# Seven products of block sums in place of eight, in the first product of a feed-forward layer

## The chip, the core and the metric

The kernel runs on one core of a Trainium2 chip. The core has a matrix engine (TensorE; PE in the profile, and PEld for its weight loads), a vector engine (VectorE, DVE), a scalar engine (ScalarE, ACT), a general engine (GpSimd, POOL) and a sync engine (SyncE, SP), which here issues the large transfers. Each engine works through its own queue in order; they wait for each other by semaphores. The metric is the device time of one execution in microseconds (us), as the median of several runs.

## The reference

A trunk of two pre-norm residual layers works on 256 tokens of 2048 dimensions, in float32. Layer 0 mixes tokens by retention and neighbourhood attention, layer 1 by differential attention. Each layer then has cross-attention into 256 memory tokens and a gated feed-forward block (FFN). Only the FFN bears on the change:

```python
D_MODEL = 2048
SEQ = 256
FFN_HIDDEN = -((-8 * D_MODEL) // (3 * 256)) * 256   # 5632

def swiglu_ffn(h, w_in, w_out):
    g, u = jnp.split(h @ w_in, 2, axis=-1)
    return (jax.nn.silu(g) * u) @ w_out
...
x = x + swiglu_ffn(rms_norm(x, norm_ffn_g[i]), w_ffn_in[i], w_ffn_out[i])
```

So per layer the first product is 256 x 2048 times 2048 x 11264 (gate and up, 5632 columns each), and the second 256 x 5632 times 5632 x 2048.

## The kernel before, in words

**Units.** All large products are cut in the same way. The columns of a weight matrix are taken in blocks of 512 (`NB`), its rows in quarters of 512. One block of one quarter, 128 partitions x 4 x 512 float32 or 1 MB, is loaded into a tile `raw` (three buffers) by one transfer on SP's queue (line 282). A unit is one half of such a tile, two row tiles of 128. `prepare` (line 269) makes each unit's two operands: ScalarE writes the rounded high part `wh` (line 292), VectorE the remainder `wl` (line 293), each 128 x 1024. `wh` and `wl` have three buffers each, and `LOOK = 2` lets `prepare` run two units ahead of the matmuls.

**Matmuls.** `gemm` (line 297) runs the units in the order that `plan` holds. For one unit it does 12 matmuls of 128 x 128 by 128 x 512: for two halves of the tokens (`t`), two row tiles (`j`), and three terms, high x high, high x low and low x high (lines 321 to 323). A block of the first FFN product takes 8 units (the 16 row tiles of 2048 dimensions) and accumulates into two PSUM banks, one for each half of the tokens; then `epi` is called. PSUM has eight banks: pools `ps_acc` (four, tags `acc0` and `acc1`), `ps_t` (two, tag `pt`) and `ps_a` (two, tag `pa`).

**FFN.** The 11 hidden blocks go in three groups of 4, 4 and 3 (`FFN_GROUPS`). In each group the first product alternates a gate block and an up block; `epi_in` (line 841) applies SiLU to the gate block on ScalarE (line 847) and multiplies the up block into it on VectorE (line 850). The result is turned by `act_T` (line 830): VectorE transposes 32 x 32 squares (line 389), SP writes it to a DRAM scratch (`zd`, line 391), POOL reads it back regrouped (line 394), and ScalarE and VectorE split it into high and low parts `aT` (lines 429 and 430). Then comes the group's second product. In the first group of a layer the first four blocks run together (`by_rows`, line 229; `wide`), quarter by quarter, since the normalized input `hTf` is itself still being turned: block 0 of it by matmul transposes (`feed_turns`, line 399), blocks 1 to 3 by the same path through DRAM (`feed`, line 409; blocks 2 and 3 use the tiles `qT` and `kT` of the attention stage, which are free in the FFN).

**Order.** Work beside the units is written as small generators that `Side` steps through after each unit (`pump`), or at once when a unit needs them (`drain`, through `gate`). That is the order in which the program writes instructions. A scheduler then lays out each engine's queue, SP's transfers among them.

Of the kernel before, what the change touches and what calls it, by code (L numbers as in the profile page):

```python
# [16 lines left out]
P = 128  # L17
# [64 lines left out]
def trunk_kernel(  # L82
# [181 lines left out]
    units = [(i, b, u) for i, ph in enumerate(plan) for b, u in ph[3]]  # L264
    ahead = deque()
    raws = {}
    at = {"unit": 0, "phase": 0}

    def prepare():

        i, b, u = units[at["unit"]]
        w2, rows, cols, _ = plan[i]
        c, h = u // 2, u % 2
# [22 lines left out]

    def gemm(kts, src, epi, gate=None, steps=1, wide=False):
        hi, lo = src
# [4 lines left out]
        for b, u in order:  # L303
            side.drain((gate or {}).get(u, ()))
            if b not in accs:
                pools = ((ps_acc, f"acc{t}") for t in range(2))
# [4 lines left out]
            while len(ahead) <= LOOK and at["unit"] < len(units):  # L311
                prepare()
            wh, wl = ahead.popleft()
            acc = accs[b]
            first, left[b] = left[b] == nu, left[b] - 1
            last = left[b] == 0
            for t in range(2):
                ts = slice(t * P, (t + 1) * P)
                for j in range(2):
                    kt = kts[u // 2] + 2 * (u % 2) + j  # L320
                    nc.tensor.matmul(acc[t], lhsT=hi[:, kt, ts], rhs=wh[:, j], start=first and j == 0, stop=False)  # L321
                    nc.tensor.matmul(acc[t], lhsT=hi[:, kt, ts], rhs=wl[:, j], start=False, stop=False)  # L322
                    nc.tensor.matmul(acc[t], lhsT=lo[:, kt, ts], rhs=wh[:, j], start=False, stop=last and j == 1)  # L323
            if last:
                epi(b, acc)
            side.pump(steps)

    def rsqrt_mean(dst, ss, n):
# [48 lines left out]
    def regroup(srcs, room=""):  # L377
# [5 lines left out]
        elif room:  # L383
            zt, zT = (qk.tile([P, 4 * T], F32, tag=room + x, name="zz") for x in "hl")
        else:
# [12 lines left out]

    def feed_turns(dst, b, u, srcs, gi, layer, ssr):

# [4 lines left out]
        square_sum(ssr[0][:, u, b:b + 1], srcs[u])  # L405
        return
        yield

# [69 lines left out]
    def turned(name):  # L478
        return tuple(qk.tile([P, 4, T], F32R, name=name + x) for x in "hl")

# [278 lines left out]
    for layer in range(2):  # L759
# [57 lines left out]
        ssr = new_ss("ssx")  # L817
        tasks = []

        def epi_xo(b, acc):  # L820
            add_x(acc, b)
            if b == 0:
                tasks.extend(side.add(feed_turns(hT, b, u, x_block(b), 3, layer, ssr), u) for u in range(2))
            else:
# [11 lines left out]
        for g0, g1 in FFN_GROUPS:  # L836
# [3 lines left out]

            def epi_in(i, acc):
# [11 lines left out]

            gemm(KT4, hT, epi_in, gate=gate, wide=g0 == 0)
            gate = None
# [55 lines left out]
```

## Time and profile before

| | before |
|---|---|
| median of 3 runs (range) | 2474.95 us (2474.5 to 2476.11) |
| profiled execution: time / span of its instructions | 2475.84 us / 2474.1 us |
| PE busy, matmuls | 2456.3 us, 11184 |
| PEld busy | 2037.1 us |
| DVE busy | 1475.7 us |
| ACT busy | 1187.0 us |
| mean granted TensorE clock | 1.000 |
| read from HBM | 486.88 MB, 206 GB/s over the span |

The span runs from the first to the last instruction of the profiled execution; 1.7 us of that execution's time lie around it. Busy time of an engine is the time in which at least one of its instructions runs. A matmul's shown duration is longer than the distance to the next one, since matmuls overlap; the distance of their starts is the rate. The same holds, to a smaller degree, for VectorE and ScalarE: instructions with no wait between them start a little before the one ahead of them has ended.

### The profile page before, as it was taken

The numbers are of one execution on the slowest core, as the hardware profiler recorded it, in microseconds if no ns is written. First come the engines' busy times: TensorE is split into PE (matmuls) and PEld (weight loads), VectorE is DVE, ScalarE is ACT, GpSimd is POOL, SyncE is SP. The second block draws the span as 40 slices with busy tenths as digits, with TensorE's granted clock in tenths as the row PEclk, the third lists the DMA queues.
The fourth block names the chain that finished last, engine by engine and source line by source line (L and its number), as shares of the span: only waits on it lengthen the run. The fifth ranks groups of instructions, "written<-read, shape, count | busy, mean of one in ns | idle before, by whom it ended". The sixth has DMA issues, their size and how long they took to land.

```text
span 2474.1 us, 28641 instructions
## 1 busy us (share of the span) xinstructions
PE 2456.3 (99%) x11184; PEld 2037.1 (82%) x11184; DVE 1475.7 (60%) x1833; ACT 1187.0 (48%) x1538; POOL 138.2 (6%) x215
## 2 busy tenths in 40 slices
PE   8999999999999999999999999999999999999999
PEld 6888888888888888888888888888888888888887
DVE  6775565675655555555567766767655545555554
ACT  6554464564443444444455555655544444443443
POOL 1000001010000000000010000010100000000000
PEclk9999999999999999999999999999999999999999
DMA  8555567656765666566674555675766656665665
GB/s 288 177 169 179 175 226 245 214 192 213 233 216 200 205 212 225 194 198 226 225 241 164 170 170 168 212 249 171 237 222 210 215 188 214 228 206 200 207 217 175
DMA packets 250184, 511.82 MB, mean 207 GB/s; under 512 B 11328, under 2 KB 11968, under 8 KB 250048
## 3 DMA queue, kind: packets, MB, share of 16 engines
q1 hardware_dynamic: 239568, 484.47, 58.5%
q0 software_dynamic: 8320, 23.08, 4.1%
q10 hardware_dynamic: 2160, 2.44, 0.3%
q8 instruction: 87, 1.43, 0.2%
q14 instruction: 49, 0.40, 0.0%
HBM read 486.88 MB, written 23.07 MB: 206 GB/s over the span
## 4 chain that ended last, share of the span: by engine, by line
PE 92%; DMA 3%; DVE 3%; ACT 1%; POOL 1%; issue 0%; ACTq 0%; SPq 0%; POOLq 0%; DVEq 0%
PE acc L322 30%; PE acc L321 30%; PE acc L323 30%; DMA zz<-zd 2%; DVE wl L293 1%; DMA zd<-zz 1%; PE pt L345 1%; ACT wh L292 0%; PE pt L545 0%; PE pa_s L437 0%; PE pa_s L436 0%; DVE x_sb L741 0%; PE pa_s L435 0%; POOL zz L394 0%; PE pa_r L595 0%
## 5 line engine op out<-in xcount | busy, mean ns | idle before, releaser
L293 DVE TENSOR_TENSOR wl<-raw,wh 128x1024 fp32r<-128x1024 f32 (+1 forms) x865 | 1053.7, 1221 | 870.8 <-ACT wh L292 870.4
L292 ACT CAST wh<-raw 128x1024 fp32r<-128x1024 f32 (+1 forms) x865 | 909.1, 1051 | 1158.2 <-PE acc L323 1132.8
L322 PE MATMUL acc<-wl,hTfh 128*128 128x512 f32 x1408 | 547.9, 389 | 0.6 <-DVE wl L293 0.6
L323 PE MATMUL acc<-wh,hTfl 128*128 128x512 f32 x1408 | 547.7, 389 | 0.0
L321 PE MATMUL acc<-wh,hTfh 128*128 128x512 f32 x1408 | 547.7, 389 | 0.0
L321 PE MATMUL acc<-wh,hTh 128*128 128x512 f32 x832 | 332.0, 399 | 9.8 <-ACT wh L292 8.3
L322 PE MATMUL acc<-wl,hTh 128*128 128x512 f32 x832 | 325.7, 391 | 0.9 <-DVE wl L293 0.9
L323 PE MATMUL acc<-wh,hTl 128*128 128x512 f32 x832 | 325.8, 392 | 0.0
L322 PEld LDWEIGHTS acc<-wl,hTfh 128*128 128x128 f32 x1408 | 264.3, 188 | 56.2 <-DVE wl L293 1.4
L323 PEld LDWEIGHTS acc<-wh,hTfl 128*128 128x128 f32 x1408 | 264.3, 188 | 54.9
L321 PEld LDWEIGHTS acc<-wh,hTfh 128*128 128x128 f32 x1408 | 264.3, 188 | 54.9
L322 PE MATMUL acc<-wl,aTh 128*128 128x512 f32 x704 | 274.0, 389 | 0.2 <-DVE wl L293 0.2
L323 PE MATMUL acc<-wh,aTl 128*128 128x512 f32 x704 | 273.9, 389 | 0.0
L321 PE MATMUL acc<-wh,aTh 128*128 128x512 f32 x704 | 273.9, 389 | 0.0
L321 PEld LDWEIGHTS acc<-wh,hTh 128*128 128x128 f32 x832 | 157.2, 189 | 40.0 <-ACT wh L292 8.3
L323 PEld LDWEIGHTS acc<-wh,hTl 128*128 128x128 f32 x832 | 156.7, 188 | 34.0
L322 PEld LDWEIGHTS acc<-wl,hTh 128*128 128x128 f32 x832 | 157.2, 189 | 31.2 <-DVE wl L293 1.8
L394 POOL DMA_DIRECT2D zz<-zd x160 | 87.3, 552 | 1589.9 <-DMA zd<-zz 1410.9
L322 PEld LDWEIGHTS acc<-wl,aTh 128*128 128x128 f32 x704 | 132.1, 188 | 28.2 <-DVE wl L293 0.8
L321 PEld LDWEIGHTS acc<-wh,aTh 128*128 128x128 f32 x704 | 132.1, 188 | 27.5
L323 PEld LDWEIGHTS acc<-wh,aTl 128*128 128x128 f32 x704 | 132.1, 188 | 27.3
L321 PE MATMUL acc<-wh,oTh 128*128 128x512 f32 x256 | 100.2, 392 | 0.0
(189 smaller groups left out, 1940.3 us busy)
## 6 DMA issues: line engine op xcount, KB each, us to landing
raw<-in_w_ffn_in SPq DMA_DIRECT2D x176, 1024.0 KB, 5.1
raw<-in_w_ffn_out SPq DMA_DIRECT2D x88, 1024.0 KB, 5.1
raw<-in_w_in_ab SPq DMA_DIRECT2D x55, 1024.0 KB, 5.2
raw<-in_w_in_c SPq DMA_DIRECT2D x48, 1024.0 KB, 5.2
zd<-zz SPq DMA_DIRECT2D x40, 512.0 KB, 3.8
zz<-zd POOLq DMA_DIRECT2D x160, 128.0 KB, 5.4
raw<-in_w_out_ab SPq DMA_DIRECT2D x16, 1024.0 KB, 5.1
raw<-in_w_xkv SPq DMA_DIRECT2D x16, 1024.0 KB, 5.0
```

Of the source, the lines that this page charges most:

```text
L292: nc.scalar.copy(wh[:, js], raw[:, rs])
L293: nc.vector.tensor_sub(wl[:, js], raw[:, rs], wh[:, js])
L321: nc.tensor.matmul(acc[t], lhsT=hi[:, kt, ts], rhs=wh[:, j], start=first and j == 0, stop=False)
L322: nc.tensor.matmul(acc[t], lhsT=hi[:, kt, ts], rhs=wl[:, j], start=False, stop=False)
L323: nc.tensor.matmul(acc[t], lhsT=lo[:, kt, ts], rhs=wh[:, j], start=False, stop=last and j == 1)
L345: nc.tensor.transpose(pt[:, j, t * P:(t + 1) * P], srcs[t][:, c:c + P], ident)
L394: nc.gpsimd.dma_start(zT[32 * j:32 * j + 32].rearrange("a (i n) -> a i n", i=4), zd[:, :, j].rearrange("i a n -> a i n"))
```

## The change

In a gate block and its up block, one quarter of the 2048 dimensions (the first 512 rows of the weights) is no longer multiplied as eight products of half of the tokens x 256 dimensions x 512 columns, but as seven. The 2 x 2 blocks are: rows of A, the two halves of the tokens; columns of A and rows of B, the even and the odd row tiles of the quarter; columns of B, the gate block and the up block. The form is Strassen's in Winograd's order: four sums of blocks of A (`s1` to `s4`), four of B (`t1` to `t4`), seven products, and sums of the products. It is used for all pairs except the four blocks that run together at the start of a layer: two, four and three pairs in the groups of a layer, 18 in all.

- `by_pairs` gives the order: of the twelve usual units that a pair keeps, two come first, then seven products alternate with seven units, then the last three units.
- `load_seven` loads the quarter of gate and of up, 1 MB each, into the tiles `qT` and `kT` in place of `raw`; these tiles, two of 4 KB per partition each before, become one of 8 KB. The two loads are written six and four units ahead of the pair's first product, counted in units of `prepare`.
- `prepare_seven` makes `wh` and `wl` for each of the seven products, and, after four of them, one block difference in place in the loaded tile, on VectorE.
- `seven` does six matmuls for a product. Three products add into the pair's own accumulators, four have a bank each. Pairs change sides: one has its accumulators in the four banks of `ps_acc` and the single products in `ps_t` and `ps_a`, the next the other way round.
- `combine` takes the single products out of PSUM at three points: one ScalarE copy and four VectorE additions for a pair. `epi_in` then adds them to the two accumulators of each block, four more VectorE additions, before SiLU and the product.
- `feed_turns` has a second step: for block 0 of the normalized input it makes the sums `s1` to `s4` and splits them into high and low parts, once a layer, which all pairs of the layer use.

```diff
+    def by_pairs(nblocks, lead):
+        seq = by_rows(lead, lead) if lead else []
+        for b in range(lead, nblocks, 2):
+            std = [(b + x, 2 * c + h) for c in (1, 2, 3) for x in range(2) for h in range(2)]
+            seq += std[:2]
+            for p in range(7):
+                seq += [(b, ("seven", p)), std[2 + p]]
+            seq += std[9:]
+        return seq
...
-            phase(w_ffn_in[layer], K4, cols, by_rows(n, 4) if g0 == 0 else None)
+            phase(w_ffn_in[layer], K4, cols, by_pairs(n, 4 if g0 == 0 else 0))
...
+    for n, (i, b, u) in enumerate(units):
+        if u == ("seven", 0):
+            sevens[n - 6], sevens[n - 4] = (i, b, 0), (i, b, 1)
...
+    def load_seven(i, b, x):
+        w2, rows, cols, _ = plan[i]
+        raw = seven_raw[x] = qk.tile([P, 4, NB], F32, tag=("qT", "kT")[x], name="raw7")
+        nc.sync.dma_start(raw, w2[rows[0]:rows[0] + 512, cols[b + x]:cols[b + x] + NB].rearrange(
+            "(k p) n -> p k n", p=P))
+    def prepare_seven(p):
+        (b11, b21), (b12, b22) = ([r[:, :, j] for j in range(2)] for r in (
+            seven_raw[x].rearrange("p (h j) n -> p h j n", j=2) for x in range(2)))
+        t1, t3, t2, t4 = b11, b12, b22, b21
+        src = (b11, b22, b21, t1, t3, t2, t4)[p]
+        wh = hip.tile([P, 2, NB], F32R, name="wh")
+        wl = lop.tile([P, 2, NB], F32R, name="wl")
+        nc.scalar.copy(wh, src)
+        nc.vector.tensor_sub(wl, src, wh)
+        if p == 0:
+            nc.vector.tensor_sub(t1, b12, b11)
+        elif p == 1:
+            nc.vector.tensor_sub(t3, b22, b12)
+        elif p == 3:
+            nc.vector.tensor_sub(t2, b22, t1)
+        elif p == 4:
+            nc.vector.tensor_sub(t4, b21, t2)
...
+    def seven(p, b, accs, weights, src, sums, places):
+        wh, wl = weights
+        name = ("p1", "p3", "p2", "p5", "p7", "p6", "p4")[p]
...
+        for h in range(2):
...
+            nc.tensor.matmul(acc, lhsT=lh, rhs=wh[:, h], start=own and h == 0, stop=False)
+            nc.tensor.matmul(acc, lhsT=lh, rhs=wl[:, h], start=False, stop=False)
+            nc.tensor.matmul(acc, lhsT=ll, rhs=wh[:, h], start=False, stop=own and h == 1)
+    def combine(b, u):
...
+        if (b % 2, u) == (1, 2):
+            first = new()
+            nc.scalar.copy(first, pure["p1"])
...
+        elif (b % 2, u) == (1, 5):
+            u2, v = new(), new()
+            add(u2, pure["p6"], combined[0][0])
+            add(v, pure["p5"], u2)
...
+        elif (b % 2, u) == (0, 6):
+            u3 = combined[0][1]
+            add(u3, pure["p7"], u3)
+            w = new()
+            add(w, pure["p5"], u3)
...
-    def feed_turns(dst, b, u, srcs, gi, layer, ssr):
+    def feed_turns(dst, b, u, srcs, gi, layer, ssr, sums):
...
+        a = att.tile([P, 2, T], F32, tag="att", name="parts")
+        for j in range(2):
+            nc.scalar.activation(a[:, j], pt[:, j], AF.Copy, scale=gain(gi, layer, 4 * b + 2 * u + j))
+        (a11, a21), (a12, a22) = ([a[:, j, t * P:(t + 1) * P] for t in range(2)] for j in range(2))
...
+        nc.vector.tensor_tensor(s1, a21, a22, op=ALU.add)
+        nc.vector.tensor_tensor(s2, s1, a11, op=ALU.subtract)
+        nc.vector.tensor_tensor(s3, a11, a21, op=ALU.subtract)
+        nc.vector.tensor_tensor(s4, a12, s2, op=ALU.subtract)
+        sums[u] = tuple(pp.tile([P, 4, P], F32R, tag="p" + x, name="s" + x) for x in "hl")
+        split(*sums[u], s)
...
-        return tuple(qk.tile([P, 4, T], F32R, name=name + x) for x in "hl")
+        both = qk.tile([P, 2, 4, T], F32R, tag=name, name=name)
+        return both[:, 0], both[:, 1]
...
+                if more:
+                    for t in range(2):
+                        nc.vector.tensor_tensor(more[t], acc[t], more[t], op=ALU.add)
+                    acc = more
```

More of the change, by code (lines that the diff above doesn't have):

```diff
@@ L267, in trunk_kernel @@
     at = {"unit": 0, "phase": 0}
+    seven_raw = {}
+    def load_seven(i, b, x):
[20 more added lines that the diff above has]
+            nc.vector.tensor_sub(t4, b21, t2)
+        ahead.append((wh, wl))
+        at["unit"] += 1
     def prepare():
         i, b, u = units[at["unit"]]
+        if at["unit"] in sevens:
+            load_seven(*sevens[at["unit"]])
+        if isinstance(u, tuple):
+            prepare_seven(u[1])
+            return
         w2, rows, cols, _ = plan[i]
@@ L295, in prepare, with bank, gemm @@
         at["unit"] += 1
-    def gemm(kts, src, epi, gate=None, steps=1, wide=False):
+    BANKS = (((ps_acc, "acc0"), (ps_acc, "acc1")) * 2, ((ps_t, "pt"),) * 2 + ((ps_a, "pa"),) * 2)
+    def bank(place, name):
+        return place[0].tile([P, NB], F32, tag=place[1], name=name)
+    def gemm(kts, src, epi, gate=None, steps=1, wide=False, sums=None):
         hi, lo = src
@@ L304, in gemm @@
             side.drain((gate or {}).get(u, ()))
-            if b not in accs:
+            pair = sums is not None and b >= (4 if wide else 0)
+            home = (b // 2 + (not wide)) % 2
+            if pair and b not in accs:
+                accs[b] = [bank(BANKS[home][2 * (b % 2) + t], f"acc{t}") for t in range(2)]
+                left[b] = 6
+            elif b not in accs:
                 pools = ((ps_acc, f"acc{t}") for t in range(2))
@@ L313, in gemm @@
             wh, wl = ahead.popleft()
+            if isinstance(u, tuple):
+                seven(u[1], b, accs, (wh, wl), src, sums, BANKS[1 - home])
+                continue
             acc = accs[b]
-            first, left[b] = left[b] == nu, left[b] - 1
+            first, left[b] = left[b] == (6 if pair else nu), left[b] - 1
             last = left[b] == 0
@@ L323, in gemm, with add, new @@
                     nc.tensor.matmul(acc[t], lhsT=lo[:, kt, ts], rhs=wh[:, j], start=False, stop=last and j == 1)
+            if pair:
+                combine(b, u)
             if last:
-                epi(b, acc)
+                epi(b, acc, *((combined[b % 2],) if pair else ()))
             side.pump(steps)
+    pure, combined = {}, {}
+    def seven(p, b, accs, weights, src, sums, places):
+        wh, wl = weights
+        name = ("p1", "p3", "p2", "p5", "p7", "p6", "p4")[p]
+        if name in ("p1", "p5", "p7", "p6"):
+            acc = pure[name] = bank(places[("p1", "p5", "p7", "p6").index(name)], name)
+        else:
+            acc = {"p2": accs[b][0], "p4": accs[b][1], "p3": accs[b + 1][0]}[name]
+        for h in range(2):
+            k, t = {"p1": (0, 0), "p2": (1, 0), "p4": (1, 1)}.get(name, (0, 0))
+            if name in ("p1", "p2", "p4"):
+                lh, ll = (x[:, 2 * h + k, t * P:(t + 1) * P] for x in src)
+            else:
+                lh, ll = (x[:, {"p5": 0, "p6": 1, "p7": 2, "p3": 3}[name]] for x in sums[h])
+            own = name in pure
+            nc.tensor.matmul(acc, lhsT=lh, rhs=wh[:, h], start=own and h == 0, stop=False)
+            nc.tensor.matmul(acc, lhsT=lh, rhs=wl[:, h], start=False, stop=False)
+            nc.tensor.matmul(acc, lhsT=ll, rhs=wh[:, h], start=False, stop=own and h == 1)
+    def combine(b, u):
+        def add(dst, acc, other):
+            nc.vector.tensor_tensor(dst, acc, other, op=ALU.add)
+        def new():
+            return att.tile([P, NB], F32, tag="att", name="us")
+        if (b % 2, u) == (1, 2):
+            first = new()
+            nc.scalar.copy(first, pure["p1"])
+            combined[0] = [first]
+        elif (b % 2, u) == (1, 5):
+            u2, v = new(), new()
+            add(u2, pure["p6"], combined[0][0])
+            add(v, pure["p5"], u2)
+            combined[0].append(u2)
+            combined[1] = [v]
+        elif (b % 2, u) == (0, 6):
[3 more added lines that the diff above has]
+            add(w, pure["p5"], u3)
+            combined[1].append(w)
+            pure.clear()
     def rsqrt_mean(dst, ss, n):
@@ L383, in regroup @@
         elif room:
-            zt, zT = (qk.tile([P, 4 * T], F32, tag=room + x, name="zz") for x in "hl")
+            both = qk.tile([P, 2, 4 * T], F32, tag=room, name="zz")
+            zt, zT = both[:, 0], both[:, 1]
         else:
@@ L818, in trunk_kernel @@
         tasks = []
+        sums = {}
         def epi_xo(b, acc):
@@ L822, in epi_xo @@
             if b == 0:
-                tasks.extend(side.add(feed_turns(hT, b, u, x_block(b), 3, layer, ssr), u) for u in range(2))
+                tasks.extend(side.add(feed_turns(hT, b, u, x_block(b), 3, layer, ssr, sums), u) for u in range(2))
             else:
@@ L839, in trunk_kernel, with epi_in @@
             sgs, atasks = {}, []
-            def epi_in(i, acc):
+            def epi_in(i, acc, more=None):
                 blk = i // 2
                 r1 = ssr[1]
+                if more:
+                    for t in range(2):
+                        nc.vector.tensor_tensor(more[t], acc[t], more[t], op=ALU.add)
+                    acc = more
                 if i % 2 == 0:
@@ L852, in epi_in @@
                 atasks.append(side.add(act_T(aT, sgs[blk], 4 * blk)))
-            gemm(KT4, hT, epi_in, gate=gate, wide=g0 == 0)
+            gemm(KT4, hT, epi_in, gate=gate, wide=g0 == 0, sums=sums)
             gate = None
```

6 lines of the change are left out of this document (4 added, 2 removed).

## The prediction

> **What bounds the kernel now.** I read the page's busy times and the chain of waits first, then the groups of instructions in one stage where the change acts undisturbed (805 to 979 us: layer 0, second group, first product), then single rows in time.
>
> ```profile
> span 2474.1 us, 28641 instructions
> PE 2456.3 (99%) x11184; PEld 2037.1 (82%) x11184; DVE 1475.7 (60%) x1833; ACT 1187.0 (48%) x1538; POOL 138.2 (6%) x215
> PE 92%; DMA 3%; DVE 3%; ACT 1%; POOL 1%; issue 0%; ACTq 0%; SPq 0%; POOLq 0%; DVEq 0%
> ```
>
> The matrix engine is the bound: 92% of the chain that ended last is matmuls. A matmul taken away is time, as long as VectorE and ScalarE keep up. The matmuls' rate and VectorE's rows at the end of an up block:
>
> ```profile
> 846.09 0.39 PE L321 MATMUL acc<-wh,hTfh 128*128 128x512 f32 x1
> ...
> 848.81 0.39 PE L321 MATMUL acc<-wh,hTfh 128*128 128x512 f32 x1
> ```
>
> These two are the first matmuls of two neighbouring units, 12 matmuls apart: 2.72 us, or 0.2267 us each (0.39 is a duration, not the rate).
>
> ```profile
> 849.01 1.06 ACT L292 CAST wh<-raw 128x1024 fp32r<-128x1024 f32 x1 [1.67 <-PE acc L323]
> 851.73 1.06 ACT L292 CAST wh<-raw 128x1024 fp32r<-128x1024 f32 x1 [1.66 <-PE acc L323]
> ```
>
> ```profile
> 847.38 1.22 DVE L293 TENSOR_TENSOR wl<-raw,wh 128x1024 fp32r<-128x1024 f32 x1 [1.49 <-ACT wh L292]
> 848.52 1.40 DVE L850 SCALAR_TENSOR_TENSOR sg<-acc,ssxr,sg 128x512 f32<-128x512 f32 x2
> 849.84 1.29 DVE L389 STREAM_TRANSPOSE zz<-sg 128x512 f32<-128x512 f32 x2
> 851.05 1.18 DVE L293 TENSOR_TENSOR wl<-raw,wh 128x1024 fp32r<-128x1024 f32 x1
> 852.82 1.22 DVE L293 TENSOR_TENSOR wl<-raw,wh 128x1024 fp32r<-128x1024 f32 x1 [0.58 <-ACT wh L292]
> ```
>
> Each cast starts 0.2 us after a unit starts: it waited for the matmuls of the unit before to free the third `wh`. It is for the unit two ahead, whose first matmul with `wl` comes 5.44 + 0.23 = 5.67 us after that start. In the quiet case (unit at 851.53, `wl` ended at 854.04) it is there after 2.51 us, 3.2 us early. Behind an up block's last work (848.81, ended 852.23) it is there after 3.4, 2.3 early. So in the matrix engine's view the cover is two units' length, and VectorE is what uses it up. Its whole load in that stage:
>
> ```profile
> L293 DVE TENSOR_TENSOR wl<-raw,wh 128x1024 fp32r<-128x1024 f32 x65 | 79.5, 1223 | 85.1 <-ACT wh L292 85.1
> L850 DVE SCALAR_TENSOR_TENSOR sg<-acc,ssxr,sg 128x512 f32<-128x512 f32 x6 | 4.2, 743 | 0.0
> L389 DVE STREAM_TRANSPOSE zz<-sg 128x512 f32<-128x512 f32 x6 | 3.9, 685 | 0.0
> L430 DVE TENSOR_TENSOR aTl<-zz,aTh 128x512 fp32r<-128x512 f32 x6 | 3.9, 685 | 0.0
> L741 DVE TENSOR_TENSOR x_sb<-acc,x_sb 128x512 f32<-128x512 f32 x2 | 1.3, 682 | 0.0
> ```
>
> **The change, term by term. Matmuls.** A pair has 16 units of 12, 192 matmuls. In the quarter that changes, 4 units or 48 become 7 products of 6, 42. Six fewer in each of 18 pairs (2 + 4 + 3, two layers): 108 x 0.2267 = 24.5 us. The shapes are the same (128 x 128 by 128 x 512), so I use the same rate.
>
> **VectorE and ScalarE in a pair.** The four units' `wl` become seven (+3), four block differences of 128 x 1024 come in, four additions in `combine` and four in `epi_in`, 128 x 512 each with one operand in PSUM, as in the row of line 741. No row has the difference of two float32 blocks written back as float32; the nearest is line 293 with the same size, 1.22 us. How much closer than their durations such instructions follow each other without a wait:
>
> ```profile
> 562.02 2.36 DVE L293 TENSOR_TENSOR wl<-raw,wh 128x1024 fp32r<-128x1024 f32 x2
> ```
>
> Two of 1.23 in 2.36, so the second started after 1.13 us. In the same way the rows above give 0.66 for line 850 and 0.60 for lines 389, and I take 0.60 for an addition of 0.68. Per pair VectorE then has 23 x 1.13 + 8 x 0.60 + 2 x 0.66 + 4 x 0.60 = 34.5 us, in 186 x 0.2267 = 42.2 us of matmuls: 82%, where it had 21.8 of 43.5 (50%). ScalarE gets three casts and one copy more, about 4 us, and stays near 60%. On average both are covered. What matters is the burst.
>
> Inside the stretch where products and units alternate, two neighbours last 1.36 + 2.72 = 4.08 us, so a `wl` must be there 4.31 us after its buffer came free instead of 5.67; the quiet 2.51 leaves 1.8. In 28.6 us VectorE has 18 operations of 1.13, four additions and the two of line 430: 23.9 us. Queued work is caught up there, slowly.
>
> At the joint between two pairs it is worst. After the last unit come two additions, two of line 850 and two transposes, 1.2 + 1.32 + 1.2 = 3.7 us, of which 0 to 0.5 fits in before that unit ends. Then follow `wl` of the next pair's first product, its difference, and `wl` of the unit behind it, 3 x 1.13. That last one is ready 3.5 to 3.9 + 3.4 = 6.9 to 7.3 us after the pair's start; it is wanted at 2 x 2.72 + 1.36 + 0.23 = 7.03. With whole durations and no overlap it would be 0.2 + 2 x (0.68 + 0.74 + 0.69) + 3 x 1.22 = 8.1, 1.1 late. So 0 to 1.1 us each at the joints inside a group, six a layer, 12 in all; I take 0.3, the upper end by the overlapped rows: 3.6 us. At a group's first pair the work ahead is that of `add_x` or of a usual block, shorter by 1.2 or more, and I count nothing.
>
> **Start of the FFN.** The second step of `feed_turns` runs twice a layer. The nearest rows:
>
> ```profile
> 548.89 2.19 DVE L421 SCALAR_TENSOR_TENSOR hTfl<-zz,gcol,hTfh 128x128 fp32r<-128x128 f32 x8
> ```
>
> Eight 128 x 128 operations in 2.19 us (0.27 each) and line 430's 0.60 give 4 x 0.27 + 0.60 = 1.7 us on VectorE, 3.4 a layer, and 2 x 0.4 + 0.6 on ScalarE. VectorE has no room there:
>
> ```profile
> 535.00:540.00 5.00, 5.00 (x24) 4.14 (x23) 5.00 (x8) 3.53 (x8) 0.02 (x1) 1.00 0.71 258
> 540.00:545.00 5.00, 5.00 (x24) 4.14 (x23) 4.97 (x7) 3.02 (x6) 2.20 (x4) 1.00 0.94 324
> ```
>
> (After a window's length come the busy times of PE, PEld, VectorE, ScalarE and POOL.) What stands behind this work are the transposes of blocks 1 to 3, whose way through DRAM ends here:
>
> ```profile
> 563.30 0.50 PE L322 MATMUL acc<-wl,hTfh 128*128 128x512 f32 x1 [0.27 <-DVE wl L293]
> ```
>
> That wait is there already, so most of 3.4 us moves the matmuls; bounds 0 and 3.4 a layer. I take 3, for the chain is busy from 535 on: 6 us in all.
>
> **Transfers.** A pair loads the same 8 MB. SP's queue gets two of them in another place, into tiles without a second buffer: the next pair's gate quarter can go out only when `wl` of this pair's last product is done, 2.5 us after the matmuls two units ahead of that product start. It is wanted by a cast 1.36 + 2.72 + 1.36 + 4 x 2.72 = 16.3 us after that start; a load takes
>
> ```profile
> raw<-in_w_ffn_in SPq DMA_DIRECT2D x176, 1024.0 KB, 5.1
> 16.00:20.00 4.00, 4.00 (x20) 3.30 (x19) 3.83 (x12) 2.28 (x5) 2.82 (x5) 1.00 1.05 387
> ```
>
> 5.1 us alone, and 2.7 more for each megabyte ahead of it at the 387 GB/s of the busiest stretch. That is covered with over 5 us to spare, if nothing else is held up (first rival). The up quarter's tile comes free two products earlier. The pair's banks change sides; the last single products are read after the pair's ninth usual unit, and the next pair's first matmul comes three units, 8 us, later. The merged tiles in the attention stages change no operation; nothing.
>
> **Sum**, against the profiled execution's 2475.84 us (span 2474.1 and 1.7 around it): 2475.84 - 24.5 + 6.0 + 3.6 = 2461. That execution was 0.9 above the median of the runs shown, 2474.95, so 2460.
>
> **Rivals. First, SP's queue is held up (slower).** If the next pair's gate quarter stands on SP's queue where the program writes it, it is directly ahead of the load for the pair's ninth usual unit. Let the product whose end frees it be prepared at time 0: the gap opens 2.55 us later, that load is issued 0.4 later, lands 5.1 + 2.7 later at 10.7, and cast and `wl` end at 13. The unit wanted `wl` at 5.67: 7.3 us lost at each of 12 joints, 88 us, 2548 us. [...] Against it stands where loads are in the queue now:
>
> ```profile
> 821.43 27.57 SPq L282 DMA_DIRECT2D raw<-in_w_ffn_in  x6
> 851.16 0.34 SPq L391 DMA_DIRECT2D zd<-zz  x1
> 854.07 5.81 SPq L282 DMA_DIRECT2D raw<-in_w_ffn_in  x2
> ```
>
> The last of the six ends at 849.00, 0.4 us after the `wl` of 847.38 had ended and freed its buffer. It is for a unit seven ahead of 846.09, written by the program five units after the write to `zd` at 851.16, and it stands before it. So the queue holds transfers in the order in which they can start. By that, the ninth unit's load, whose buffer is free since the pair's first third, stands well ahead. Seven in 100.
>
> In this rival the matrix engine would also sit idle for 7 us at a time, and the start of the trace shows what an idle start costs:
>
> ```profile
> 10.51 0.63 PE L321 MATMUL acc<-wh,hTh 128*128 128x512 f32 x1
> 13.07 0.63 PE L321 MATMUL acc<-wh,hTh 128*128 128x512 f32 x1
> 14.32 0.39 PE L321 MATMUL acc<-wh,hTh 128*128 128x512 f32 x1
> ```
>
> Six matmuls took 2.56 us there, 0.43 each, twelve in all at 0.2 us too much: 2.4 us a gap, 29 more, 2577. [...]
>
> **Second, VectorE decides in each pair (no change).** With whole durations a pair costs VectorE 23 x 1.22 + 8 x 0.68 + 2 x 0.74 + 4 x 0.69 = 37.7 of 42.2 us, and with 1.1 us lost at each of 12 joints and 3.4 a layer at the start the sum is 2475.84 - 24.5 + 13.2 + 6.8 - 0.9 = 2470. If besides the joints each of the 18 pairs loses another 0.5 us in its stretch, it is 2479. For it: the stretch has only 1.8 us in reserve. Against: instructions in a row do overlap in every such row. Twenty in 100, and eight more for worse of this kind (2485 and over, a mean loss of 2 us a pair).
>
> **Third, all of it is hidden**: 2475 - 24.5 = 2450.5. At the start of the FFN the extra work would have to fall into VectorE's idle time behind 550 us. Ten in 100.
>
> **How the numbers follow.** The forecast, 2453 to 2468, has 55 in 100, the third rival 10, the second 20 (half of it under 2470), worse of its kind 8, the first 7. A measurement of this kernel tells about 0.2%, 5 us. Faster than that (under 2470): 55 + 10 + 10 - 3 for the forecast's own tail = 0.72. Within it: the other half of the second and that tail, 0.13. Slower: 8 + 7 = 0.15. The range is from everything hidden, 2450, to a joint loss near the upper bound with something lost in the stretches, 2476; outside it are the first rival and the worse part of the second.
>
> **What would show it.** Matmuls fall by 108 to 11076; VectorE gets 15 instructions more a pair and 20 in the two layers, 1833 + 290 = 2123; ScalarE 4 a pair and 12, 1538 + 84 = 1622. VectorE's busy time rises by 18 x (7 x 1.22 + 8 x 0.68) + 8 = 260 us to about 1736. Right: matmuls of the pairs at 0.2267 us with waits for `wl` under a microsecond, at the third unit behind a joint; one wait of 2 to 4 us near 563. The first rival would show as ScalarE waiting for a transfer of `raw` some 7 us near each pair's end and SP's waits there; the second as `wl` waits spread over the stretches with VectorE busy over 95% in them. Wrong in size: if the waits of the matmuls for `wl` sum to over 20 us, or to nothing.

## The result and the profile after

The changed kernel takes 2451.26 us (median of 4 runs, 2450.77 to 2452.37), the kernel before took 2474.76 on the same chip (2474.5 to 2476.11): a ratio of 0.9905, 95% interval 0.9887 to 0.9922. The saving is 23.5 us of the 24.5 that 108 matmuls are worth. The forecast of 2460 us was 8.7 too high, and the time lies under the 2453 to 2468 that had 55 in 100; the case that came true is the third rival, all of it hidden, at 2450.5 us.

The head of the page after, with the busy times of the engines and the chain that ended last:

```profile
span 2450.3 us, 28849 instructions
PE 2433.0 (99%) x11076; PEld 2016.7 (82%) x11076; DVE 1707.8 (70%) x2123; ACT 1256.8 (51%) x1622; POOL 139.4 (6%) x215
PE 96%; DMA 2%; DVE 2%; ACT 0%; POOL 0%; issue 0%; ACTq 0%; SPq 0%; DVEq 0%; POOLq 0%
```

The counts are those forecast: 11076 matmuls, 2123 instructions on VectorE, 1622 on ScalarE. VectorE's busy time is 28 us under the 1736 forecast. That sum took whole durations, while the busy time counts instructions that overlap only once: with 1.13 us for a block operation and 0.60 for an addition, a pair adds 7 x 1.13 + 8 x 0.60 = 12.7 us, 18 pairs 229, and the measured rise is 1707.8 - 1475.7 = 232, the sums at the start of the FFN among it.

How long one FFN takes can be read from the first matmul on the normed input and the last on the activations. Layer 0, before and then after (the columns behind the count are durations in ns, then the first and the last start in us):

```profile
L321 PE MATMUL acc<-wh,hTfh x704: 388/389/389, 543.6 to 1196.3; 128*128 128x512 f32 x176
L321 PE MATMUL acc<-wh,aTh x352: 388/389/393, 718.2 to 1262.1; 128*128 128x512 f32 x176
```

```profile
L386 PE MATMUL acc<-wh,hTfh x560: 388/389/398, 543.6 to 1184.4; 128*128 128x512 f32 x187
L386 PE MATMUL acc<-wh,aTh x352: 387/389/396, 715.9 to 1250.5; 128*128 128x512 f32 x176
```

1262.1 - 543.6 = 718.5 us became 1250.5 - 543.6 = 706.9: 11.6 of the 54 x 0.2267 = 12.2 us that the matmuls of one layer are worth. So 0.6 us was given back in this layer, where the forecast had 3 at the start and 6 x 0.3 at the joints.

VectorE and the matrix engine of the changed kernel at a joint between two pairs (start, duration):

```profile
844.88 1.28 DVE L975 TENSOR_TENSOR us<-acc,us 128x512 f32<-128x512 f32 x2
846.08 1.41 DVE L983 SCALAR_TENSOR_TENSOR sg<-us,ssxr,sg 128x512 f32<-128x512 f32 x2
847.40 1.30 DVE L504 STREAM_TRANSPOSE zz<-sg 128x512 f32<-128x512 f32 x2
848.62 1.18 DVE L304 TENSOR_TENSOR wl<-raw,wh 128x1024 fp32r<-128x1024 f32 x1
849.73 1.21 DVE L345 TENSOR_TENSOR wl<-raw,wh 128x1024 fp32r<-128x1024 f32 x1
850.86 1.22 DVE L306 TENSOR_TENSOR raw<-raw,raw 128x1024 f32<-128x1024 f32 x1
```

```profile
852.15 0.39 PE L387 MATMUL acc<-wl,hTfh 128*128 128x512 f32 x1
```

The durations are those of the forecast. The order is not: the third unit's `wl` (line 345) stands ahead of the first product's block difference (line 306), not behind it. It ends at 850.94 and is wanted at 852.15: 1.2 us early, and no matmul waits.

In the execution of the changed kernel taken later beside other runs (2450.71 us, below) one whole pair reads as follows; behind the window's length stand the busy times of PE, PEld, VectorE, ScalarE and POOL, the granted clock, the DMA share and GB/s:

```profile
852.00:894.20 42.20, 42.20 (x188) 34.96 (x187) 35.72 (x38) 22.85 (x25) 2.18 (x4) 1.00 0.65 225
```

The matrix engine has no idle time in it. VectorE is busy for 35.7 of 42.2 us (34.5 were worked out).

### The profile page after: what moved, and what is told of

Read it like the earlier page. It is cut to its first block, busy times and chain, and to the rows that moved or that the text cites. A ratio compares the mean times of both kernels' runs of the same rounds, so it can differ in the third digit from the quotient of the medians.

```text
span 2450.3 us, 28849 instructions
## 1 busy us (share of the span) xinstructions
PE 2433.0 (99%) x11076; PEld 2016.7 (82%) x11076; DVE 1707.8 (70%) x2123; ACT 1256.8 (51%) x1622; POOL 139.4 (6%) x215
## 4 chain that ended last, share of the span: by engine, by line
PE 96%; DMA 2%; DVE 2%; ACT 0%; POOL 0%; issue 0%; ACTq 0%; SPq 0%; DVEq 0%; POOLq 0%
PE acc L386 28%; PE acc L387 28%; PE acc L388 28%; PE p L414 1%; PE p L412 1%; PE p L413 1%; PE acc L414 1%; PE acc L412 1%; PE acc L413 1%; PE pt L459 1%; DMA zz<-zd 1%; DVE wl L345 0%; DMA zd<-zz 0%; PE pt L673 0%; PE pa_s L564 0%; PE pa_s L563 0%
## 5 line engine op out<-in xcount | busy, mean ns | idle before, releaser
L345 DVE TENSOR_TENSOR wl<-raw,wh 128x1024 fp32r<-128x1024 f32 (+1 forms) x793 | 964.6, 1220 | 541.9 <-ACT wh L344 534.1
L344 ACT CAST wh<-raw 128x1024 fp32r<-128x1024 f32 (+1 forms) x793 | 833.3, 1052 | 894.2 <-PE acc L388 812.5
L387 PE MATMUL acc<-wl,hTfh 128*128 128x512 f32 x1120 | 436.4, 390 | 0.4 <-DVE wl L345 0.4
L388 PE MATMUL acc<-wh,hTfl 128*128 128x512 f32 x1120 | 435.8, 389 | 0.0
L386 PE MATMUL acc<-wh,hTfh 128*128 128x512 f32 x1120 | 435.1, 389 | 0.0
L387 PEld LDWEIGHTS acc<-wl,hTfh 128*128 128x128 f32 x1120 | 210.2, 188 | 46.5 <-DVE wl L345 2.9
L386 PEld LDWEIGHTS acc<-wh,hTfh 128*128 128x128 f32 x1120 | 210.2, 188 | 43.6
L388 PEld LDWEIGHTS acc<-wh,hTfl 128*128 128x128 f32 x1120 | 210.2, 188 | 43.5
L303 ACT CAST wh<-raw 128x1024 fp32r<-128x1024 f32 x126 | 133.0, 1055 | 185.7 <-PE acc L388 171.1
L304 DVE TENSOR_TENSOR wl<-raw,wh 128x1024 fp32r<-128x1024 f32 x126 | 153.5, 1219 | 71.6 <-ACT wh L303 71.3
```

The source lines that it names most:

```text
L303: nc.scalar.copy(wh, src)
L304: nc.vector.tensor_sub(wl, src, wh)
L344: nc.scalar.copy(wh[:, js], raw[:, rs])
L345: nc.vector.tensor_sub(wl[:, js], raw[:, rs], wh[:, js])
```

## The experiments

Times are compared with the kernel before, run in turn on the same chip, and with the changed kernel's control run:

| run | us | kernel before beside it | ratio, 95% interval |
|---|---|---|---|
| changed kernel, first | 2451.26 | 2474.76 | 0.9905, 0.9887 to 0.9922 |
| changed kernel, control | 2450.71 | 2474.94 | 0.9907, 0.9891 to 0.9924 |
| sums only | 2475.29 | 2475.34 | 1.0000, 0.9991 to 1.0009 |
| sums twice | 2485.10 | 2475.34 | 1.0038, 1.0023 to 1.0053 |
| sums three times | 2491.34 | 2475.34 | 1.0063, 1.0046 to 1.0080 |
| difference ahead | 2453.64 | 2475.34 | 0.9914, 0.9900 to 0.9927 |
| load behind | 2561.44 | 2475.34 | 1.0347, 1.0333 to 1.0361 |
| three low parts twice | 2458.28 | 2474.94 | 0.9936, 0.9922 to 0.9951 |
| seven low parts twice | 2489.80 | 2474.00 | 1.0069, 1.0049 to 1.0089 |
| six products in a row | 2466.71 | 2474.94 | 0.9969, 0.9958 to 0.9980 |
| second product too | 2446.24 | 2475.34 | 0.9884, 0.9870 to 0.9897 |
| second product, sums later | 2443.02 | 2474.94 | 0.9874, 0.9860 to 0.9889 |

The control's own expectation, and what separates two executions of one program:

> The changed kernel itself once more, beside the others on the same chip, so that differences of a few us can be read: 2451 us, with no wait at the third unit behind a joint.

```profile
L386 PE MATMUL acc<-wh,hTfh x560: 388/389/398, 543.7 to 1184.2; 128*128 128x512 f32 x187
L386 PE MATMUL acc<-wh,aTh x352: 389/389/389, 715.7 to 1249.5; 128*128 128x512 f32 x176
```

Its FFN of layer 0 takes 1249.5 - 543.7 = 705.8 us, 1.1 less than in the first execution: here 12.7 us are saved, all that the matmuls are worth. Differences of a microsecond in a layer are therefore no evidence by themselves; where the text below speaks of tenths, they repeat at every joint of one trace.

### The start of the FFN: the sums alone

```diff
 # the kernel before
-    def feed_turns(dst, b, u, srcs, gi, layer, ssr):
+    def feed_turns(dst, b, u, srcs, gi, layer, ssr, sums):
...
+        a = att.tile([P, 2, T], F32, tag="att", name="parts")
...
+        nc.vector.tensor_tensor(s1, a21, a22, op=ALU.add)
...
+        split(*sums[u], s)
```

> The kernel before with one part of the change alone: the second step of feed_turns, which makes the block sums of the first quarter (two scaled copies on ScalarE, four adds and a split on VectorE, for each half), at the start of each FFN. The sums are made and used by nothing; all units stay the usual ones. By the step 'start of the FFN' of the prediction the 3 us of extra VectorE work in each layer delay the refill of blocks 1 to 3 and TensorE with it: 2474.8 + 6.0 = 2481 us. By the rival that cover is there for all of it (the traces show the writes of the trips through DRAM 2 us later, the reads of block 2 not later): 2475 us, at most 0.4 us more.

Nothing, 2475.29 against 2475.34. The wait near 563 us that the forecast expected to grow by 3 us is hardly longer than the 0.27 us of before:

```profile
564.00 0.50 PE L322 MATMUL acc<-wl,hTfh 128*128 128x512 f32 x1 [0.31 <-DVE wl L293]
```

The work is there, and VectorE's time is used. The first two windows of this stage stand in the prediction for the kernel before; its next two, and the same two of the changed kernel:

```profile
545.00:550.00 5.00, 5.00 (x24) 4.14 (x23) 4.49 (x11) 3.91 (x10) 1.54 (x3) 1.00 0.93 309
550.00:555.00 5.00, 5.00 (x24) 4.14 (x23) 3.55 (x8) 2.37 (x4) 2.88 (x6) 1.00 1.00 285
```

```profile
545.00:550.00 5.00, 5.00 (x23) 4.13 (x22) 5.00 (x8) 2.87 (x6) 0.85 (x2) 1.00 0.97 308
550.00:555.00 5.00, 5.00 (x24) 4.13 (x23) 4.75 (x12) 3.28 (x7) 2.31 (x5) 1.00 0.95 285
```

VectorE's busy time rises by 0.51 + 1.20 = 1.7 us between 545 and 555. Over both layers it rises by 6.0 us with the sums alone (1481.7 against 1475.7), 3.0 a layer where 3.4 was worked out: the small operations follow each other after 0.20 us, not 0.27. So over half of the work was pushed into idle time there, as the third rival had it. The transposed blocks are written out 2.1 to 2.9 us later, but the way through DRAM is shorter when they are. The wait near 563 hangs on block 2; these are the issue of its write to DRAM and the first work of ScalarE on what came back, before and then with the sums alone:

```profile
541.06 0.34 SPq L391 DMA_DIRECT2D zd<-zz  x1
559.34 1.71 ACT L419 ACTIVATE hTfh<-zz,gcol 128x256 fp32r<-128x256 f32 x4 [3.60 <-DMA zz<-zd]
```

```profile
543.45 0.34 SPq L391 DMA_DIRECT2D zd<-zz  x1
560.03 1.71 ACT L431 ACTIVATE hTfh<-zz,gcol 128x256 fp32r<-128x256 f32 x4 [3.63 <-DMA zz<-zd]
```

The write goes out 2.4 us later and the block is there 0.7 us later, so 1.7 us come back on the way. Why the later trip is shorter is not shown.

### How much cover the start has

The same sums made twice, and with `range(3)` three times, in a row:

```diff
 # in the kernel with the sums alone
-        a = att.tile([P, 2, T], F32, tag="att", name="parts")
+        for _ in range(2):
+            a = att.tile([P, 2, T], F32, tag="att", name="parts")
...
-        split(*sums[u], s)
+            split(*sums[u], s)
```

> The kernel before with the block sums of the first quarter made twice over at the start of each FFN (6.8 us of VectorE a layer) and used by nothing. Made once they cost nothing that could be measured. If VectorE's delay goes on to the matmuls one for one, as the prediction took it, and once was hidden by a cover of about its own size, the second time costs all of its 3.4 us in each layer: 2475 + 6.8 = 2482 us. If the way of the blocks through DRAM (20 us for the second block) is what sets the wait there, and gets shorter when its write comes later, about half of it: 2478 us, with a wait of 1 to 2 us near 564 us. If cover is left over: 2475 us.

> The same with the sums made three times over (10.2 us of VectorE a layer). One for one beyond the first time: 2475 + 13.6 = 2489 us. With the way through DRAM taking half of it: 2482 us. With cover left over for twice but not for three times: 2482 us at the most.

Dearer than any of these: +9.8 and +16.0 us. The second making is 2.9 us of VectorE's busy time in each layer (1487.4 us in all, against 1481.7) and cost 4.9 us; the third cost 3.1. The wait did not come where it was expected, near 564, but at the FFN's first unit. Matmuls with the sums made twice (the bracket is the idle time before, and what ended it):

```profile
544.85 0.47 PE L321 MATMUL acc<-wh,hTfh 128*128 128x512 f32 x1
545.56 0.51 PE L321 MATMUL acc<-wh,hTfh 128*128 128x512 f32 x1 [0.24 <-DVE x_sb L754]
548.48 0.65 PE L322 MATMUL acc<-wl,hTfh 128*128 128x512 f32 x1 [2.41 <-DVE wl L293]
...
551.91 0.48 PE L322 MATMUL acc<-wl,hTfh 128*128 128x512 f32 x1
```

From 544.85 to 548.48 the matmuls are two steps apart, for which 0.45 us would do: 3.2 us are lost to `x_sb` and to a `wl` that stands behind the sums on VectorE. Then eight steps take 3.43 us to 551.91, 0.43 each instead of 0.2267: 1.6 us more, at half the granted clock (its row stands in the last section). So what the sums were first to run into was the two units' cover of the first `wl`, and it just held for them once: in the run with the sums alone its weight load waits 0.34 us at 544.59, and the matmuls lose 0.2. The second 2.9 us of work bought 3.2 us of delay and a dip of the clock.

### The joint: the difference ahead

```diff
 # prepare(), in the changed kernel; at["diff"] is the last block difference
+            diff = at.pop("diff", None)
+            with tc.issue_after(diff.ins) if diff is not None else ExitStack():
                 nc.vector.tensor_sub(wl[:, js], raw[:, rs], wh[:, js])
```

> The changed kernel, with each block difference forced on VectorE ahead of the next usual unit's low part, as the prediction took it to stand; the trace of the changed kernel has it behind that low part at 12 joints. By the step 'joint' of the prediction the third unit's low part is then late by 0.3 us at each of 12 joints: 2451.3 + 3.6 = 2454.9 us, and waits of about 0.3 us at the third unit behind each joint. By the reading of the changed kernel's trace the low part is 1.2 us early there and a difference takes 1.13 us, so 0.1 us is left over: 2451.3 us, no wait. If the difference ahead also pushes the low parts behind it, 12 x 1.1 = 13 us more: 2464 us.

This is the order that the prediction had assumed. VectorE and the matmuls at the same joint as above:

```profile
850.50 1.22 DVE L306 TENSOR_TENSOR raw<-raw,raw 128x1024 f32<-128x1024 f32 x1
851.64 1.22 DVE L347 TENSOR_TENSOR wl<-raw,wh 128x1024 fp32r<-128x1024 f32 x1
```

```profile
852.58 0.39 PE L388 MATMUL acc<-wh,hTfh 128*128 128x512 f32 x1
852.91 0.50 PE L389 MATMUL acc<-wl,hTfh 128*128 128x512 f32 x1
853.25 0.40 PE L390 MATMUL acc<-wh,hTfl 128*128 128x512 f32 x1
```

`wl` now ends at 852.86 and was wanted 0.2267 us behind 852.58, at 852.81. The two distances, 0.33 and 0.34, are 0.1 too long each: 0.21 us lost, and the same stands at all six joints inside the groups of that layer. Twelve times that is 2.5 us; the time rose by 2453.64 - 2450.71 = 2.9 us. The intervals of the two ratios overlap, so the time alone would not settle it. The view of waits has no line for it on the matrix engine, since the wait falls on the weight load ahead of the matmul. That line for layer 0 from 640 to 1250 us (total, times, longest; six at the joints, the seventh in a second product); the changed kernel's control has none there:

```profile
PEld acc L389 <- DVE wl L347: 2.6, 7, 0.4
```

The prediction's price for a joint was 0.3 us, and with the order that it assumed it is 0.2. What was wrong was the order. That the price came so near is in part luck: the prediction charged the time by which `wl` is late, and that is 0.05 us; the rest is that two distances lengthen.

At the first pair of an FFN, where the prediction counted nothing, the assumed order does stand in the changed kernel's queue, and `wl` is late there. In the control:

```profile
637.02 1.22 DVE L345 TENSOR_TENSOR wl<-raw,wh 128x1024 fp32r<-128x1024 f32 x1
```

```profile
638.29 0.50 PE L387 MATMUL acc<-wl,hTfh 128*128 128x512 f32 x1
```

`wl` ends at 638.24; the matmul comes 0.28 us behind the one at 638.01, and the next follows after 0.34. That is 0.16 us lost, in each layer.

### The first rival: the load behind

```diff
 # prepare(), in the changed kernel
-        if at["unit"] in sevens:
-            load_seven(*sevens[at["unit"]])
+        seven_load = load_seven(*sevens[at["unit"]]) if at["unit"] in sevens else None
...
+            elif seven_load is not None:
+                with tc.issue_after(seven_load.ins):
+                    nc.sync.dma_start(raw, src)
```

> The changed kernel, with one order on SP's queue: the usual weight load that is asked for in the same step as the second-next pair's first special load (the ninth unit's load) must be issued behind that special load, so that it waits for the buffer that the special load waits for. By the first rival of the prediction the ninth unit is then 7.3 us late at each of 12 joints: 2451 + 88 = 2539 us, and with the clock falling in the gaps up to 2568 us. If the load still lands in time behind the special one, 2451 us.

2561.44 us, 110.7 more than the control. So the mechanism is real and its price was nearly right; only its condition is not met in the changed kernel. SP's queue of the changed kernel (special loads are line 291, usual ones line 334), then of this one:

```profile
655.90 0.37 SPq L291 DMA_DIRECT2D raw<-in_w_ffn_in  x1
657.26 0.37 SPq L334 DMA_DIRECT2D raw<-in_w_ffn_in  x1
659.98 0.37 SPq L291 DMA_DIRECT2D raw<-in_w_ffn_in  x1
```

```profile
656.50 4.45 SPq L291 DMA_DIRECT2D raw<-in_w_ffn_in  x2
661.00 1.06 SPq L334 DMA_DIRECT2D raw<-in_w_ffn_in  x2
```

In the changed kernel a usual load goes out between the two special ones. The first special load is the up quarter's: it holds the queue for 6.0 us, until the sixth product's `wl` has freed its tile, and the usual load stands behind it. It loses nothing by that, since its own buffer comes free only with a `wl` that VectorE begins at 656.01 and ends at 657.24. Behind the gate quarter's load, which waits for the seventh product's `wl`, it does not stand. With the order forced, two special loads take 4.45 us of the queue, and the usual load goes out at 661.0 instead of about 657.3. What follows on ScalarE and on the matrix engine:

```profile
668.33 1.99 ACT L346 CAST wh<-raw 128x1024 fp32r<-128x1024 f32 x2 [9.03 <-DMA raw<-in_w_ffn_in]
```

```profile
663.26 0.39 PE L416 MATMUL acc<-wh,hTfl 128*128 128x512 f32 x1
669.43 1.22 PE L388 MATMUL acc<-wh,hTfh 128*128 128x512 f32 x2 [5.78 <-ACT wh L346]
```

```profile
668.00:672.00 4.00, 2.53 (x5) 1.62 (x6) 2.36 (x2) 2.96 (x3) 0.00 (x0) 0.50 1.05 388
```

The start at 669.43 is 5.9 us late, and the matmuls behind it lose another 2.4 us, at a granted clock of 0.50. All twelve joints look like this: 5.9 to 6.9 us late, and 2.4 to 3.5 more behind it, some 109 us of the 111. The prediction had 7.3 and 2.4. In SP's rows the usual load behind the two special ones goes out 0.05 us after them, at 661.00, so here it did wait for what they waited for; where it stands in the queue decided.

### How near VectorE is to deciding

The low part of some of the seven products is computed a second time into a tile that nothing reads; without the condition it is done for all seven.

```diff
 # prepare_seven(p), in the changed kernel
         nc.vector.tensor_sub(wl, src, wh)
+        if p in (0, 2, 4):
+            nc.vector.tensor_sub(m8.tile([P, 2, 4 * T], F32, tag="m8", name="twice")[:, :, 0:NB], src, wh)
```

> The changed kernel, with the low part of three of the seven products (the first, third and fifth) computed a second time into a tile that nothing reads: 3.4 us more VectorE a pair. By the account over a whole pair of the prediction (VectorE 34.7 of 42.2 us, then 38.1) nothing waits: 2451 us. By the account over the stretch of the seven products, where VectorE runs without a gap and is 1.2 us early, 2.2 us a joint are lost: 2451 + 12 x 2.2 = 2477 us, to 2491 us if it is so in all 18 pairs.

> The changed kernel, with the low part of all seven products computed a second time into a tile that nothing reads: 7 x 1.13 = 7.9 us more VectorE a pair. With three of them twice (3.4 us) each of the 12 joints lost 0.5 us, so the cover there is about 2.9 us. By the account over the stretch of the seven products each pair then loses 7.9 - 2.9 = 5.0 us, 18 pairs 90 us: 2541 us. By the account over a whole pair (VectorE 34.7 + 7.9 = 42.6 of 42.2 us) 0.4 us a pair: 2458 us, or what three twice gave, if that was something else.

Neither account holds. Three twice cost 7.6 us against the control, seven twice 39. In the traces each joint inside a group loses 0.4 us with three (the distances of the matmuls' starts beyond 0.2267, summed) and 2.6 with seven; the first pair of an FFN loses 1.9 and 1.0 (layers 0 and 1) with three. The whole-pair account had 0 and 0.4 a pair; the account over the stretch 2.2 and 5.0. The wait that counts with seven, and VectorE around it:

```profile
880.11 0.50 PE L389 MATMUL acc<-wl,hTfh 128*128 128x512 f32 x1 [1.32 <-DVE wl L347]
```

```profile
877.71 1.21 DVE L314 TENSOR_TENSOR raw<-raw,raw 128x1024 f32<-128x1024 f32 x1
878.84 1.22 DVE L347 TENSOR_TENSOR wl<-raw,wh 128x1024 fp32r<-128x1024 f32 x1
```

The last wait of a pair is for the `wl` that stands behind the fourth and last block difference. Up to there VectorE works without a gap, and only what is added up to there costs: three doubled low parts, 3.4 us, or five, 5.7 us. 3.4 - 0.4 and 5.7 - 2.6 give the same cover, 3.0 to 3.1 us at a joint, and beyond it the loss is one for one. This reading was formed on these two runs and no third tests it. It also holds for their order only: the scheduler laid VectorE's queue out anew. In the changed kernel the fourth difference (line 312 there) stands well ahead:

```profile
858.81 1.22 DVE L312 TENSOR_TENSOR raw<-raw,raw 128x1024 f32<-128x1024 f32 x1
```

There the low part nearest to being late is that of the fourth usual unit, which starts on VectorE at 854.26, ends at 855.48 and is wanted at 856.23: 0.75 us early. So in the order that these two runs got, the change was 3 us of VectorE work in each joint's stretch away from the second rival, two and a half block operations; in its own order the tightest `wl` has 0.75 us.

### What the alternation is worth

```diff
 # by_pairs(), in the changed kernel
-            seq += std[:2]
-            for p in range(7):
-                seq += [(b, ("seven", p)), std[2 + p]]
-            seq += std[9:]
+            seq += std[:2] + [(b, ("seven", 0)), std[2]]
+            seq += [(b, ("seven", p)) for p in range(1, 7)] + std[3:]
```

> The changed kernel, with the last six of the seven products in a row instead of each between two usual units; the same work on each engine. By the account over a whole pair nothing changes: 2451 us. By the account over the stretch: the six need 6 low parts and 3 differences, 9 x 1.13 = 10.2 us of VectorE, for 6 x 1.36 = 8.2 us of TensorE, so 2 us a pair are lost less what the buffers are ahead, to 4 us with ScalarE's copies between: 2487 to 2523 us for 18 pairs.

2466.71 us: 16 us of the 24.5 are lost, less than half of what the account over the stretch had. The matrix engine's largest new wait (total, times, longest) is not for VectorE:

```profile
PE acc L410 <- ACT wh L301: 7.4, 12, 0.6
```

```profile
906.53 1.05 ACT L301 CAST wh<-raw 128x1024 fp32r<-128x1024 f32 x1 [1.48 <-DVE raw L310]
```

It is for ScalarE's cast of a block difference, and the cast waited for that difference on VectorE. With a usual unit between two products this chain of two engines has 2.72 us more to run; in a row it shows, once in 12 of the 18 pairs, and the rest of the 16 us is waits of some tenths for `wl`.

### The same products in the FFN's second product

Since everything was covered, the same seven products were put into the second product of the groups of four blocks: for each pair of output column blocks the first block's four K tiles, with the block sums of the activations made where that block is split.

```diff
 # plan, act_T, gemm and epi_out, in the changed kernel
-            phase(w_ffn_out[layer], tuple(b * NB for b in range(g0, g1)), four, woven(4, n, n - 2))
+            phase(w_ffn_out[layer], tuple(b * NB for b in range(g0, g1)), four,
+                  by_pairs(4, 0) if g1 - g0 == 4 else woven(4, n, n - 2))
...
+            if osums is not None:
+                both = m8.tile([P, 2, 2, 4, P], F32R, tag="m8", name="osum")
+                for h in range(2):
+                    (a11, a21), (a12, a22) = ([zT[:, :, 2 * h + j, t] for t in range(2)] for j in range(2))
...
+                    osums[h] = (both[:, 0, h], both[:, 1, h])
+                    split(*osums[h], s)
...
-            home = (b // 2 + (not wide)) % 2
+            home = (b // 2) % 2
...
+                if more:
+                    add_x(more, b)
```

> The changed kernel with the same seven products for eight also in the FFN's second product of the groups of four blocks: the first block's four K tiles for each pair of output column blocks, 2 pairs in 2 groups in 2 layers, so 8 pairs of 6 matmuls fewer each (48 x 0.2267 = 10.9 us). The block sums of the activations are made where their block is split (eight adds and two splits on VectorE in each of 4 groups, about 3 us each). If all of it is covered as in the first product: 2451.3 - 10.9 = 2440.4 us. If the sums delay the units behind them, 4 x 3 = 12 us are given back: 2452 us. If the special loads at the seams between the two products find the queue held up, 8 x 7 = 56 us more: 2496 us.

2446.24 us; some 5 of the 10.9 us were missing, by the ratios to the kernel before. Most of it stands in two waits, one in each layer, of which this is the first:

```profile
641.71 0.50 PE L391 MATMUL acc<-wl,hTfh 128*128 128x512 f32 x1 [2.49 <-DVE wl L346]
```

The new sums (some 3 us of VectorE) had landed in the first pair of the FFN, directly ahead of its third unit's `wl`. The cover of 3 us measured above, inside the groups, is not there: in the control this `wl` is already late. So nearly the whole work came out as a wait. The sums were then made behind the split of the activations, seven units later:

```diff
             if osums is not None:
+                yield 7
```

> The kernel with seven products in the FFN's second product too (e5_second_product, 2446.2 us, where 2440.4 were expected: its trace has one wait of 2.5 us for a low part in each layer, at 641 us, where the eight adds and two splits of the new sums stand between the low parts of the first pair). Here the sums are made seven units later, in the four usual units at the pair's end. If the waits were all that was missing: 2446.2 - 5.0 = 2441 us. If the sums only delay the low parts there instead: 2446 us. Without the waits and with none elsewhere the matmuls alone give 2451.3 - 10.9 = 2440.4 us.

2443.02 us, 7.7 below the control and 3.2 below the version before it; both waits are gone. The remaining 3 us are seven waits for `wl`, 2.7 us together and none over 0.7 (control: one of 0.3).

This version, at 0.9874 of the kernel before, beats both kernels.

## Why the prediction was right, and where it was wrong

**The matmuls.** Right: 108 fewer at 0.2267 us. In the control 24.2 of the 24.5 us arrived.

**The pair's average.** Right: 34.5 us of VectorE worked out, 35.7 measured, of 42.2; ScalarE is busy for 22.85 us of it, 54%, where near 60% was worked out.

**The joint (3.6 us).** The mechanism holds, and about the price, 0.2 us a joint where 0.3 was taken, once the order is the assumed one. The step that failed is "then follow `wl` of the next pair's first product, its difference, and `wl` of the unit behind it". At the twelve joints inside the groups the difference comes last of the three in the kernel's queue, so the term is 0. The prediction took this order from the text of the program, though for SP's queue it had argued from the profile that instructions need not stand as the program writes them.

**The start of the FFN (6.0 us).** The step that failed is "most of 3.4 us moves the matmuls". It measured 0 within 2.2 us for both layers, and the trace has 0.2 a layer at the FFN's first unit. The work itself was 3.0 us a layer and not 3.4. Two things stood against it: VectorE's idle time behind 545 us, which the prediction's windows, ending at 545, did not show, and a way through DRAM whose length is not fixed (1.7 us shorter behind a write that went out 2.4 us later). Its lower bound of 0 was the right end. Made a second time, the same work cost 4.9 us a layer: the cover was just about used up, and that it sufficed was not worked out by the prediction.

**The first rival.** Given 7 in 100, and rightly not chosen; its working gave 9.7 us a joint with the clock, and the forced order measured 9.1. That a usual load waits behind a special one was the author's assumption, which no row of the kernel before shows; the forced order shows it (0.05 us behind the special ones, at 661.00). The 2.4 us for the clock was an estimate from the start of the trace; 2.4 to 3.5 were measured. The argument from where SP's loads stood before held: the usual load stands ahead of the gate quarter's. One reading on the way was off, without effect: the up quarter's tile comes free one product earlier and not two, 4.08 us in SP's rows.

**The second rival.** Its place was right, the stretch behind a joint, and its distance was 3 us of VectorE work there, in the order of the two runs that measured it. The fear of whole durations was unfounded: block operations followed each other after 1.13 us throughout.

**The range.** Both loss terms were taken near their upper ends. With either at nothing the forecast would have been within 6 us. The measured time is 1.3 us above the lower end of the range, which holds it because the third rival was made that end. Of the prediction's own signs, the single wait of 2 to 4 us near 563 and the waits at the third unit behind a joint did not come, and the one for "wrong in size" did: the control's matmuls wait for `wl` once, for 0.3 us.

## What to carry to other kernels

Before a delay is charged to the bounding engine, look for where it is absorbed on the way: in the idle time of the delayed engine over the whole time until its result is wanted, not in the window where the work is added. A small change of order on a full engine decides tenths of a microsecond at each repeat (0.2 us at a joint here), and in what order a scheduler puts independent instructions is read from the queue, not from the program's text. A measured cover holds for its place and its order of instructions: 3 us inside a group, nothing at the first pair of an FFN. New work goes where cover is seen in the trace, as the seven units' delay of the sums had it.

## What was not expected of the hardware

**Waits with and without a dip of the clock.** With the sums made twice, a wait of 2.41 us right behind one of 0.24 was followed by matmuls at 0.43 us, in both layers. In the first version with the second product, a wait of 2.49 us behind undisturbed matmuls was followed by matmuls at full rate, also in both layers (granted clock: after the length and the five engines' busy times):

```profile
550.00:552.00 2.00, 2.00 (x6) 1.52 (x6) 2.00 (x5) 0.72 (x2) 0.00 (x0) 0.50 0.83 256
```

```profile
642.00:644.00 2.00, 2.00 (x10) 1.61 (x10) 2.00 (x3) 0.00 (x0) 0.00 (x0) 1.00 0.44 137
```

Single waits of 1.3 us with the seven low parts doubled had no dip behind them (after the one that ended at 880.11 the granted clock is 1.00 from 880 to 884 us), and the 5.8 us of the forced load cost 2.4 to 3.5 more. But with the seven low parts doubled there are also two short waits close together, 0.78 and 0.77 us with one matmul between them (0.74 and 0.77 at the same place in layer 1). From 1.3 us behind the second one on, eight matmuls run at 0.43 us, 1.6 us more, with the granted clock at half:

```profile
563.49 0.49 PE L388 MATMUL acc<-wh,hTfh 128*128 128x512 f32 x1 [0.78 <-ACT wh L346]
564.75 0.50 PE L389 MATMUL acc<-wl,hTfh 128*128 128x512 f32 x1 [0.77 <-DVE wl L347]
```

```profile
566.00:568.00 2.00, 2.00 (x6) 1.60 (x5) 2.00 (x9) 1.30 (x2) 0.00 (x0) 0.50 1.05 395
```

So the length of the longest wait alone does not decide in this kernel; what lies around it counts too, and these runs do not show how. Of the two signs the distances of the starts are the surer: from 10 to 14 us of the kernel before, the column of the granted clock says 1.00 while the matmuls start 0.43 us apart.

**A wait that no line of the matrix engine shows.** A `wl` late by 0.05 us lengthened two distances between matmuls by 0.1 us each and left no wait on the matrix engine, only one on its weight loads.
